# Where in 64 bytes the operands of the products begin: weights in one half, moving operands in the other

## The chip, the core and the metric

One core of one Trainium2 chip runs the whole kernel. The metric is the device time of one execution in microseconds, as the median of three runs. TensorE multiplies, VectorE and ScalarE do the elementwise work, GpSimd does little here, and all weights come from HBM by DMAs that SyncE issues.

## The reference

Two layers of a diffusion transformer over 256 tokens ("latents") and 256 context tokens of width 1024, in float32. Cut to what matters:

```python
for i in range(2):
    mod = silu(c) @ ada_w[i] + ada_b[i]             # six vectors; another six for the context
    h = rms_norm(x, g) * (1 + scale) + shift        # for x and for ctx
    y = even_mixer(h) if i == 0 else retention_mixer(h)
    x = x + gate * y                                # ctx likewise, in layer 0 only
    x = x + gate2 * (square(relu(h2 @ w1)) @ w2)    # h2: a second norm and modulation
return rms_norm(x, final_g)
# even_mixer: p = h @ w_in; a long convolution (by DFT products) on 3 x 512 columns,
#   attention in windows with 8 heads of 64; both @ w_out
# retention_mixer: p = h @ w_in; 4 heads, q and k of 256, v of 512, forwards and backwards;
#   o = (q k^T * decay) v, normalised, times silu(gates); @ w_out
```

## The kernel before

The tokens lie along the columns, 256 latents and then 256 context tokens; features lie across the 128 partitions. Every large product is split in two parts: a float32 operand is rounded to the type fp32r (`hi`) and the rest is kept as a second fp32r tile (`lo`), so that one product becomes three matmuls (`mm3`, line 149): hi x hi, hi x lo, lo x hi. `mm` gives TensorE a stationary operand (`lhsT`, 128 columns, loaded by an instruction of its own ahead of each matmul) and a moving one (`rhs`, 128, 256, 258 or 512 columns).

Weights arrive as 234 units of 128 x 1024 floats in the order of `unit_list`; `make_unit` (line 192) copies a raw unit into `wh` on ScalarE and the rest into `wl` on VectorE. The stages follow each other in time: the even mixer (to about 265 us; in it `hy` holds the modulated input, hi and lo tiles alike), the first MLP (`hx`, `hy` hold its input, `hid` its inner layer; 512 columns each, to about 640), the odd stage with the retention (to about 980), and the last MLP with the final norm (only the 256 latents; its input has 258 columns, since two columns carry the shift). Nearly always the weights are stationary. In the odd stage's `values` and `gates` it is the other way round: `hx`, `hy` are stationary and `wh`, `wl` move. In `scores` of the odd stage `kh`, `kl` are stationary and `qh`, `ql` move, and in `outs` `sh`, `sl` are stationary and `vh`, `vl` move. The order of instructions on TensorE is written out by hand in the mixers and around the norms; elsewhere a planner orders them by priorities.

Where a tile begins: a pool hands out addresses within a partition in the order in which its tags are first asked for, each tile rounded up to 32 bytes; the pools lie one behind the other. So every tile begins either in the first or in the second 32 of 64 bytes. In the program before, these are the halves:

- The pool `keep` (line 1428 on) has an odd number of 32-byte pieces before the pools that follow it, so `raw`, `wh`, `wl`, `nq` and the first tiles of each stage's pool begin in the second half. All tiles of the even stage that enter its fp32r products do, and all of the first MLP.
- In the odd stage `hx` and `hy` begin in the second half. The tile `lg` (8 floats, 32 bytes) turns that over for what is allocated after it: `qh`, `ql`, `kh0`, `kl0`, `kh1`, `kl1`, `vh`, `vl`, the four `sh`/`sl`, `sg` and `yth`, `ytl` begin in the first half.
- The last MLP takes its tiles from the same pool by the same tags. Its `hid` lies in `qh` to `vl`, in the first half. Its input lies in the tags of `hx`, `hy`, and there one slice of 258 floats is 1032 bytes long, so the four slices of a tile begin 32, 40, 48 and 56 bytes into their 64.

Slices of weights are 128 columns, 512 bytes, apart, so they begin in the half in which their tile does.

Of the kernel before, what the change touches and what calls it, by code (L numbers as in the profile page):

```python
# [9 lines left out]
F32 = mybir.dt.float32  # L10
F32R = mybir.dt.float32r
# [5 lines left out]
P = 128  # L17
D = 1024
KT = 8
SEQ = 256  # L20
TOK = 512
D_FF = 4096
EPS = 1e-6
# [33 lines left out]

CST = {}
_n = 0
for _name, _w in (("ident", 128), ("tneg", 2), ("wf", 2)):  # L60
    CST[_name] = (_n, _n + _w)
    _n += _w
N_CST = _n

# [63 lines left out]
class Build:  # L130
# [26 lines left out]

    def lo(self, o, x, hi, eng=None):
        return self.tt(o, x, hi.bitcast(F32), ALU.subtract, eng)

    def psm(self):
        return self.ps.tile([P, 512], F32, tag="m", name="psm", bufs=3)
# [232 lines left out]
    def norm_late(self, layer, sh, sc, h, part):  # L395


        lat = slice(0, SEQ)
        mod = self.mod[layer]
        dg = self.nq()  # L400
        self.V.memset(dg[:, SEQ : SEQ + 2], 1.0 / P)
        for i, (hi, lo) in enumerate(self.h_whole):
            x, y = (z.rearrange("p (k t) -> p k t", k=4)[:, :, SEQ:] for z in (hi, lo))
            shift = mod[:, sh, 4 * i : 4 * i + 4, :]
            self.S.copy(x, shift)
            self.lo(y, shift, x)
        with self.tc.high_priority(NORM_PRIO):
            for kt in range(KT):
                r, c = self.res[:, kt, lat], mod[:, sc, kt, 0:1]
                self.S.activation(h[kt][0][:, lat], r, AF.Copy, scale=c)  # L410
                self.V.scalar_tensor_tensor(h[kt][1][:, lat], r, c, h[kt][0][:, lat].bitcast(F32), op0=ALU.mult, op1=ALU.subtract)
        acc = self.sums(SEQ, 6)
        with self.tc.manual_schedule(engines={mybir.EngineType.PE}):
            for j in range(3):
                part(j, None, (0, 1))
            sums = self.rstd_sums(self.rstd_parts(acc, 6, lat), lat, self.psd())
            part(3, None, (0, 1))
            with self.tc.high_priority(NORM_PRIO):
                self.diagonal(self.inv_sqrt(sums, 2, D), 2, dg)
            ps = self.psn()  # L420
            self.mm(ps[:, : SEQ + 2], self.ones, dg[:, : SEQ + 2], True, True)
            self.rms = self.tmp2.tile([P, SEQ + 2], F32, tag="diff", name="rms", bufs=1)
            with self.tc.high_priority(NORM_PRIO):
                self.S.copy(self.rms, ps[:, : SEQ + 2])
# [128 lines left out]
    def mlp(self, layer, T, spread=0, pool=None):  # L553
        tc = self.tc
        with nullcontext(pool) if pool else tc.tile_pool(name="mlp", bufs=1, reuse_waits="tile") as pool:
            if layer == 0:
                self.tmp2, self.n_t2 = pool, T2_MLP
                self.cond = pool.tile([P, 2, 1024], F32, tag="cond", name="cond")
                self.nc.sync.dma_start(self.cond, self.I["ccrow"])
            TW = T if layer == 0 else T + 2  # L560
            h = self.h_tiles(pool, TW)
            self.T = T
            first = self.four()
            part = self.split_part(h, first)
            if layer == 0:
                self.norm_proj(layer, SH_M, SC_M, h, part)
            else:
                self.norm_late(layer, SH_M, SC_M, h, part)
            hid = {}
            end = self.last_mm  # L570
            if layer == 0:
                with tc.issue_after(self.last_act):
                    self.S.activation(self.cond, self.cond, AF.Silu)

            def evac(g, m, ps):
                if m == 0:
                    tags = [("hh", "hl")] * 2 if layer == 0 else MLP1_TAGS[g % 2]
                    hid[g] = [[pool.tile([P, 4 * T], F32R, tag=x, name="hid", bufs=1 if layer else 4) for x in pair] for pair in tags]
                hh, hl = hid[g][m // 4]
                sl = slice((m % 4) * T, (m % 4) * T + T)  # L580
                q = self.t2()
                if layer == 0:
                    r = self.t2()
                    self.S.activation(r[:, :T], ps[:, :T], AF.Relu)
                    self.tt(q[:, :T], r[:, :T], r[:, :T], ALU.mult)
                else:
                    self.tt(q[:, :TW], ps[:, :TW], self.rms, ALU.mult)

                def rest():
                    if layer:  # L590
                        self.S.activation(q[:, :T], q[:, :T], AF.Relu, bias=q[:, T : T + 1])
                        self.S.activation(q[:, :T], q[:, :T], AF.Square)
                    self.S.copy(hh[:, sl], q[:, :T])  # L593
                    self.lo(hl[:, sl], q[:, :T], hh[:, sl])

                return rest

            def w1(g):
                m0 = 0
                if g == 0:  # L600
                    m0 = 4
                    for rest in [evac(g, m, ps) for m, ps in enumerate(first)]:
                        rest()
                for m in range(m0, 8):
                    evac(g, m, self.proj_a(h, TW, self.psa() if layer and g == 0 and m < 6 else None))()
                    with self.tc.issue_after(end), self.tc.issue_after(self.last_lo):
                        self.more(spread)

            def w2(g):
                hs = []  # L610
                for kt in range(8):
                    hh, hl = hid[g][kt // 4]
                    sl = slice((kt % 4) * T, (kt % 4) * T + T)
                    hs.append((hh[:, sl], hl[:, sl]))
                if layer and g == 3:
                    self.final(hs)
                    return
                for m in range(6 if g == 3 else 8):
                    self.add_res(self.proj_a(hs, T), layer, G_M, m, slice(0, T))
                    self.more(SPREAD2 - m % 2)  # L620
                if g == 3:
                    self.all_adas()
                    self.tail(hs, T, layer, G_M, (6, 7))

            w1(0)
            for g in range(1, 4):
                w1(g)
                w2(g - 1)
            w2(3)

    def h_tiles(self, pool, T):
        h = []
        self.h_whole = []
        for i in range(2):
            hh = pool.tile([P, 4 * T], F32R, tag=f"hx{i}", name="hx")
            hl = pool.tile([P, 4 * T], F32R, tag=f"hy{i}", name="hy")
            self.h_whole.append((hh, hl))
            h += [(hh[:, j * T : j * T + T], hl[:, j * T : j * T + T]) for j in range(4)]
        return h


# [246 lines left out]
    def even(self):  # L888
        tc, nc, V, S, G, I = self.tc, self.nc, self.V, self.S, self.G, self.I
        with tc.tile_pool(name="even", bufs=1, reuse_waits="tile") as pool0:  # L890
# [6 lines left out]
                    return pool0.tile(shape, dt, tag=tag, name=name, bufs=self.bufs.get(tag, 1))  # L897

            pool = Sized()
            self.tmp2, self.n_t2 = pool0, T2_EVEN  # L900
            self.rope = pool.tile([P, 2, SEQ], F32, tag="rope", name="rope")
            self.mask = pool.tile([P, 2, P], BF16, tag="mask", name="mask")
# [69 lines left out]
            with tc.manual_schedule(engines={mybir.EngineType.PE}):  # L972
# [48 lines left out]
                def spectra():  # L1021

                    raw = self.raw(I["dft2"])
                    tabs.extend(pool.tile([P, 1024], F32R, tag="pt", name="dft") for _ in range(2))
                    S.copy(tabs[0], raw)
                    self.lo(tabs[1], raw, tabs[0])
                    self.all_adas()
# [38 lines left out]
            y = {}  # L1066
# [129 lines left out]
    def odd(self, stop=False):  # L1196
        tc, nc, V, S, G, I = self.tc, self.nc, self.V, self.S, self.G, self.I
        with tc.tile_pool(name="odd", bufs=1, reuse_waits="tile") as pool:
            self.tmp2, self.n_t2 = pool, T2_ODD
            h = self.h_tiles(pool, TOK)  # L1200
            rope = pool.tile([P, 6, SEQ], F32, tag="rope", name="rope1")
            nc.sync.dma_start(rope, I["rope1"])
# [1 line left out]
            nc.sync.dma_start(diff, I["diff"])  # L1204
            tri = pool.tile([P, 2, P], F32, tag="tri", name="tri")
            nc.sync.dma_start(tri, I["tri"])
            lg = pool.tile([P, 8], F32, tag="lg", name="lg")
            r0 = PAR["rate"][0]
            banks, part = self.qk_part(h)
            self.norm_proj(1, SH_A, SC_A, h, part)  # L1210
# [17 lines left out]
            def heads_qk(hd):  # L1228
# [5 lines left out]
                else:  # L1234
# [2 lines left out]
                qh = pool.tile([P, 2, 2, SEQ], F32R, tag="qh", name="qh")  # L1237
                ql = pool.tile([P, 2, 2, SEQ], F32R, tag="ql", name="ql")
                k = [
                    (pool.tile([P, 2, TOK], F32R, tag=f"kh{d}", name="kh"), pool.tile([P, 2, TOK], F32R, tag=f"kl{d}", name="kl"))  # L1240
                    for d in range(2)
                ]
                pair = lambda: self.t2().rearrange("p (a b) -> p a b", a=2)
# [36 lines left out]
            def scores(hd, q, k):  # L1280
                out = []
                for d in range(2):
# [7 lines left out]
                        blocks = [(pa, 0, 0, (0, 256), 0), (pa, 256, 1, (128, 256), 0), (pb, 0, 2, (0, 256), 256), (pb, 256, 3, (0, 256), 128)]  # L1290
                    else:
                        blocks = [(pa, 0, 0, (0, 128), 384), (pa, 128, 1, (0, 256), 256), (pb, 0, 2, (0, 256), 128), (pb, 256, 3, (0, 256), 0)]
                    sh = pool.tile([P, 896], F32R, tag=f"sh{d}", name="sh")
                    sl = pool.tile([P, 896], F32R, tag=f"sl{d}", name="sl")
                    for half in range(2):
                        s = self.t2()
                        for ps, c, kt, (q0, q1), e0 in blocks[2 * half : 2 * half + 2]:
# [122 lines left out]
    def run(self, stop=None):  # L1420
# [3 lines left out]
        with ExitStack() as es:  # L1424
# [13 lines left out]
            self.res = keep.tile([P, KT, TOK], F32, tag="res", name="res")  # L1438
            self.ones = keep.tile([P, P], F32, tag="ones", name="ones")
            V.memset(self.ones, 1.0)  # L1440
            self.eps = keep.tile([P, 1], F32, tag="eps", name="eps")
            V.memset(self.eps, EPS)
            self.csil = keep.tile([P, KT, 32], F32, tag="csil", name="csil")
            V.memset(self.csil, 0.0)
            self.nsink = keep.tile([P, 8], F32, tag="nsink", name="nsink")
# [75 lines left out]
def constants():  # L1521
# [4 lines left out]
    for t in range(2):  # L1526
        cst[:, CST["tneg"][0] + t] = -((np.arange(P) + P * t).astype(f4) / f4(SEQ))
        w = np.full(P, 2.0 / 512)
        if t == 0:
            w[0] = 1.0 / 512  # L1530
        cst[:, CST["wf"][0] + t] = w
    c["cst"] = cst

    t = np.arange(256)
# [120 lines left out]
```

## Time and profile before

| | |
|---|---|
| median of 3 runs | 1172.65 us (1171.71 to 1175.13) |
| profiled execution | 1174.92 us, span 1173.1 us |
| mean granted clock of TensorE | 0.997 |
| TensorE busy | 1146.3 us, 98%, 6922 matmuls |
| weight loads | 980.2 us, 84%, 6922 |
| VectorE busy | 797.4 us, 68% |
| ScalarE busy | 533.2 us, 45% |
| DMA | 181.77 MB, mean 155 GB/s |

A matmul's own duration in the profile reaches from its start to its modelled end, and successive matmuls overlap. The distance between their starts is what adds up; it is read from an unbroken piece of work with its count of instructions.

### The profile page before, as it was taken

The page shows a single profiled execution, that of the slowest core. Times are in us where ns is not written, and L with a number is a line of the kernel's source. Part 1 is how long each engine was busy: PE and PEld are TensorE (multiplying, and loading weights), DVE is VectorE, ACT ScalarE, POOL GpSimd, SP SyncE. Part 2 cuts the span into 40 slices and gives each one's busy share as a digit, 9 for nine tenths or more (in the row PEclk, how much of TensorE's full clock was granted, in tenths as well). Part 3 has the DMA queues.
Part 4 walks back from the last instruction along what each step waited for, and adds up shares of the span by engine and source line. Part 5 has one row for each costly group of instructions (what it writes and reads, how often), then busy time and mean ns, then how long its engine had stood idle before and what let it go on. Part 6 is the DMA issues. An engine that isn't in the chain of part 4 may idle for free.

```text
span 1173.1 us, 17557 instructions
## 1 busy us (share of the span) xinstructions
PE 1146.3 (98%) x6922; PEld 980.2 (84%) x6922; DVE 797.4 (68%) x1364; ACT 533.2 (45%) x840; POOL 33.6 (3%) x29
## 2 busy tenths in 40 slices
PE   6899999999999999999999999999999999999997
PEld 3566677789888888788889889889889889999997
DVE  5767666768999866666348847647647567766665
ACT  6455555336433132123236453453453545846544
POOL 1200000300000000000000000000000000000000
PEclk9999999999999999999999999999999999999999
DMA  8735545123676766665323343343342345555651
GB/s 305 265 91 155 187 132 172 54 73 116 213 221 213 244 205 207 198 197 179 96 88 133 112 144 109 109 143 104 112 144 73 126 125 171 185 185 183 189 186 54
DMA packets 50355, 181.77 MB, mean 155 GB/s; under 512 B 5601, under 2 KB 6177, under 8 KB 50146
## 3 DMA queue, kind: packets, MB, share of 16 engines
q1 hardware_dynamic: 49986, 180.14, 47.5%
q8 instruction: 54, 0.88, 0.3%
q10 hardware_dynamic: 288, 0.52, 0.1%
q14 instruction: 27, 0.22, 0.1%
HBM read 179.59 MB, written 1.05 MB: 154 GB/s over the span
## 4 chain that ended last, share of the span: by engine, by line
PE 85%; DMA 6%; DVE 5%; ACT 2%; issue 1%; SPq 0%; DVEq 0%; ACTq 0%
PE psm L146 65%; PE psa L146 13%; DMA raw<-in_adat 5%; PE psn L146 2%; PE psd L213 1%; DMA raw<-in_w 1%; DVE wl L156 1%; DVE ac L278 1%; DVE hy L393 1%; PE psa L1126 1%; PE psd L146 1%; PE psn L1187 1%; PE psa L1171 1%; ACT wh L198 1%; DVE t L156 1%
## 5 line engine op out<-in xcount | busy, mean ns | idle before, releaser
L198 ACT CAST wh<-raw 128x1024 fp32r<-128x1024 f32 x234 | 245.5, 1050 | 340.0 <-PE psm L146 237.9
L156 DVE TENSOR_TENSOR wl<-raw,wh 128x1024 fp32r<-128x1024 f32 x234 | 286.7, 1226 | 154.6 <-ACT wh L198 146.1
L146 PE MATMUL psm<-hy,wh 128*128 128x512 f32 (+2 forms) x952 | 304.9, 341 | 6.0 <-DVE hy L393 3.0
L146 PE MATMUL psm<-hid,wh 128*128 128x256 f32 (+1 forms) x1056 | 250.2, 330 | 0.1
L146 PE MATMUL psm<-hx,wl 128*128 128x256 f32 (+2 forms) x696 | 221.3, 318 | 0.8 <-DVE wl L156 0.8
L146 PE MATMUL psm<-hx,wh 128*128 128x256 f32 (+2 forms) x696 | 221.7, 319 | 0.1
L146 PEld LDWEIGHTS psm<-hy,wh 128*128 128x128 f32 x952 | 178.8, 190 | 28.3 <-DVE hy L393 5.2
L146 PEld LDWEIGHTS psm<-hid,wh 128*128 128x128 f32 x1056 | 178.1, 188 | 19.3 <-issue 0.5
L146 PE MATMUL psm<-hid,wl 128*128 128x256 f32 (+1 forms) x528 | 174.0, 330 | 0.3 <-DVE wl L156 0.3
L146 PEld LDWEIGHTS psm<-hx,wl 128*128 128x128 f32 x696 | 131.6, 189 | 10.2 <-DVE wl L156 1.5
L146 PEld LDWEIGHTS psm<-hx,wh 128*128 128x128 f32 x696 | 131.9, 190 | 9.5 <-ACT hx L385 0.5
L278 DVE SCALAR_TENSOR_TENSOR ac<-raw,cond 128x1024 f32<-128x1024 f32 x80 | 96.6, 1220 | 45.0 <-DMA raw<-in_adat 42.9
L146 PEld LDWEIGHTS psm<-hid,wl 128*128 128x128 f32 x528 | 99.3, 188 | 10.1 <-DVE wl L156 0.8
L484 DVE SCALAR_TENSOR_TENSOR res<-psm,mod,res 128x256 f32<-128x256 f32 x108 | 48.9, 481 | 62.2 <-PE psm L146 61.8
L146 PE MATMUL psm<-wl,hx 128*128 128x512 f32 x224 | 87.5, 391 | 0.0
L146 PE MATMUL psm<-wh,hy 128*128 128x512 f32 x224 | 87.2, 391 | 0.0
L146 PE MATMUL psm<-wh,hx 128*128 128x512 f32 x224 | 84.1, 391 | 0.0
L593 ACT CAST hid<-t 128x512 fp32r<-128x512 f32 (+1 forms) x64 | 32.5, 510 | 68.3 <-DVE t L156 67.6
L146 PE MATMUL psm<-hy,wl 128*128 128x512 f32 x128 | 50.7, 396 | 0.0
L146 PEld LDWEIGHTS psm<-wl,hx 128*128 128x128 f32 x224 | 42.1, 188 | 8.7 <-DVE wl L156 0.3
L146 PEld LDWEIGHTS psm<-wh,hy 128*128 128x128 f32 x224 | 41.9, 188 | 8.5
L146 PEld LDWEIGHTS psm<-wh,hx 128*128 128x128 f32 x224 | 41.8, 188 | 8.2
(323 smaller groups left out, 1593.9 us busy)
## 6 DMA issues: line engine op xcount, KB each, us to landing
raw<-in_w SPq DMA_DIRECT2D x234, 512.0 KB, 3.4
raw<-in_adat SPq DMA_DIRECT2D x56, 512.0 KB, 3.9
raw<-in_ada SPq DMA_DIRECT2D x40, 512.0 KB, 4.3
res<-in_x SPq DMA_DIRECT2D x4, 512.0 KB, 5.4
cond<-in_ccrow SPq DMA_DIRECT2D x1, 1024.0 KB, 5.7
rope<-in_rope SPq DMA_DIRECT2D x1, 768.0 KB, 5.3
dftraw<-in_dft SPq DMA_DIRECT2D x1, 512.0 KB, 6.7
raw<-in_dft SPq DMA_DIRECT2D x1, 512.0 KB, 4.5
```

The source lines that it names most:

```text
L146: return self.PE.matmul(o, lhsT=lhsT, rhs=rhs, start=start, stop=stop)
L156: return (eng or self.V).tensor_tensor(o, a, b, op=op)
L198: self.S.copy(hi, src)
L213: self.PE.matmul(ps[32 * j : 32 * j + 32, 0:n], lhsT=self.csil[:, kt, :], rhs=rhs, start=kt == 0, stop=kt == 7, tile_position=(0, 32 * j),)
L278: self.V.scalar_tensor_tensor(junk, src, 1.0, self.cond[:, i], op0=ALU.mult, op1=ALU.mult, accum_out=self.mod[layer][:, vec, kt, i : i + 1])
L393: self.last_lo = self.V.scalar_tensor_tensor(h[1][:, s], t[:, s], b, h[0][:, s].bitcast(F32), op0=ALU.add, op1=ALU.subtract).ins
L484: self.V.scalar_tensor_tensor(r, ps[:, s], self.mod[layer][:, vec, m, i : i + 1], r, op0=ALU.mult, op1=ALU.add)
L593: self.S.copy(hh[:, sl], q[:, :T])
L1126: self.PE.matmul(pss[u][:, cols], lhsT=self.qs[t][a][half[u], o : o + P], rhs=k[b][half[u], keys], start=i == 0, stop=i == 2 and x == 2, t ...
L1171: self.PE.transpose(pt[:, kt * P : kt * P + P], p[:, kt * P : kt * P + P], self.ident)
L1187: self.PE.matmul(ps[half[u], cols], lhsT=vz[:, kt, half[u]], rhs=turned[u][:, kt if n == 4 else kt + 2], start=i == 0, stop=i == n - 1, ti ...
```

## The change

`eps` is no longer a tile of 32 bytes in `keep` but one more column of the constants `cst` (132 to 133 columns, the same number of 32-byte pieces). A helper `pad` allocates `OFF` = 8 floats (32 bytes) and clears them on GpSimd, which moves what is allocated after it by half of 64 bytes; it is called at the head of the even, the first MLP's and the odd stage's pool, and around `sh`/`sl`. `lg` takes the place of `nsink` instead of a tile of its own. `kh` and `kl` become rows with `OFF` floats at both ends; `dft` begins `OFF` floats into its tile. `h_tiles` rounds the length of a slice up to a multiple of 16 floats.

```diff
-for _name, _w in (("ident", 128), ("tneg", 2), ("wf", 2)):
+for _name, _w in (("ident", 128), ("tneg", 2), ("wf", 2), ("eps", 1)):
...
+OFF = 8
...
+    def pad(self, pool, tag="pad"):
+        self.G.memset(pool.tile([P, OFF], F32, tag=tag, name="pad"), 0.0)
...
# norm_late
-            x, y = (z.rearrange("p (k t) -> p k t", k=4)[:, :, SEQ:] for z in (hi, lo))
+            x, y = (z.rearrange("p (k t) -> p k t", k=4)[:, :, SEQ : SEQ + 2] for z in (hi, lo))
...
# mlp, layer 0; the same call in even (ahead of rope) and in odd (ahead of h)
+                self.pad(pool)
...
# h_tiles
+        T0, T = T, (T + 15) // 16 * 16
...
-            h += [(hh[:, j * T : j * T + T], hl[:, j * T : j * T + T]) for j in range(4)]
+            h += [(hh[:, j * T : j * T + T0], hl[:, j * T : j * T + T0]) for j in range(4)]
...
# even, spectra
-                    tabs.extend(pool.tile([P, 1024], F32R, tag="pt", name="dft") for _ in range(2))
+                    tabs.extend(pool.tile([P, 1024 + OFF], F32R, tag="pt", name="dft")[:, OFF:] for _ in range(2))
...
# odd
-            lg = pool.tile([P, 8], F32, tag="lg", name="lg")
+            lg = self.nsink
...
-                    (pool.tile([P, 2, TOK], F32R, tag=f"kh{d}", name="kh"), pool.tile([P, 2, TOK], F32R, tag=f"kl{d}", name="kl"))
+                    [
+                        pool.tile([P, 2 * TOK + 2 * OFF], F32R, tag=f"{x}{d}", name=x)[:, OFF : OFF + 2 * TOK].rearrange("p (a b) -> p a b", a=2)
+                        for x in ("kh", "kl")
+                    ]
...
+                    if hd == d == 0:
+                        self.pad(pool, "pads")
                     sh = pool.tile([P, 896], F32R, tag=f"sh{d}", name="sh")
                     sl = pool.tile([P, 896], F32R, tag=f"sl{d}", name="sl")
+                    if hd == 0 and d == 1:
+                        self.pad(pool, "pade")
...
# run
-            self.eps = keep.tile([P, 1], F32, tag="eps", name="eps")
-            V.memset(self.eps, EPS)
+            self.eps = self.cst[:, CST["eps"][0] : CST["eps"][1]]
```

## Rows read from the trace of the kernel before

**Rows 1.** The page: busy time by engine, and the chain that ended last.

```profile
PE 1146.3 (98%) x6922; PEld 980.2 (84%) x6922; DVE 797.4 (68%) x1364; ACT 533.2 (45%) x840; POOL 33.6 (3%) x29
...
PE 85%; DMA 6%; DVE 5%; ACT 2%; issue 1%; SPq 0%; DVEq 0%; ACTq 0%
```

**Rows 2.** TensorE's waits, the longest first: waited for, us in total, times, longest us.

```profile
PE psa L146 <- DMA hyp<-in_hyp: 4.2, 1, 4.2
```

**Rows 3.** TensorE's groups by form: output, moving and stationary tile, shape, count, busy us, mean ns.

```profile
L146 PE MATMUL psm<-hy,wh 128*128 128x512 f32 x480 | 171.5, 399 | 5.8 <-DVE hy L393 3.0 <-ACT hy L385 2.7
...
L146 PE MATMUL psm<-hy,wl 128*128 128x512 f32 x128 | 50.7, 396 | 0.0
...
L146 PE MATMUL psm<-hid,wh 128*128 128x256 f32 x576 | 102.3, 281 | 0.0
...
L146 PE MATMUL psm<-hx,wh 128*128 128x256 f32 x240 | 68.8, 287 | 0.1
...
L146 PE MATMUL psm<-hy,wh 128*128 128x258 f32 x232 | 65.2, 281 | 0.0
...
L146 PE MATMUL psa<-qh,kh 128*128 128x256 f32 x48 | 13.7, 285 | 0.0
```

**Rows 4.** The chain in order of time: start us, length us, what, count.

```profile
292.49 152.13 PE psm L146 x671
...
655.92 4.13 PE psm L146 x18
...
668.02 4.39 PE psm L146 x19
672.41 1.42 PE psa L146 x12
...
679.57 3.45 PE psm L146 x15
...
709.73 10.19 PE psm L146 x85
719.92 8.49 PE psa L146 x72
```

**Rows 5.** Timeline in the first MLP: start us, length us, engine, what.

```profile
560.45 0.39 PE L146 MATMUL psm<-hid,wl 128*128 128x512 f32 x1
560.45 0.41 PEld L146 LDWEIGHTS psm<-hid,wh 128*128 128x128 f32 x2
```

**Rows 6.** Stretches: us, busy us of each engine, TensorE's granted clock, DMA share, GB/s.

```profile
25.00:200.00 175.00, 168.58 (x1031) 116.54 (x1030) 119.79 (x251) 89.77 (x181) 9.45 (x6) 0.99 0.49 166
292.50:352.00 59.50, 59.50 (x264) 49.23 (x264) 58.05 (x90) 24.64 (x37) 0.00 (x0) 1.00 0.72 218
352.00:381.00 29.00, 29.00 (x130) 24.01 (x129) 28.08 (x48) 8.96 (x11) 0.00 (x0) 1.00 0.69 212
528.00:617.00 89.00, 88.64 (x421) 74.69 (x421) 44.67 (x67) 26.46 (x33) 0.00 (x0) 1.00 0.38 124
1027.00:1118.00 91.00, 91.00 (x771) 91.00 (x771) 60.71 (x82) 53.50 (x81) 0.00 (x0) 1.00 0.57 186
```

**Rows 7.** The chain again, asked for three stretches of the last MLP.

```profile
998.91 29.15 PE psm L146 x243
...
1027.94 21.12 PE psm L146 x181
...
1118.93 30.10 PE psm L146 x258
```

**Rows 8.** Timeline of the start: memsets, and the first uses of `eps` and `cst`.

```profile
0.74 0.18 POOL L1449 MEMSET mod<- 128x96 f32 x1 [0.29 <-POOLq L1645]
...
2.03 0.20 ACT L704 ACTIVATE pre<-eps 128x1 f32<-128x1 f32 x1
...
3.23 0.23 DVE L920 CAST identb<-cst 128x128 bf16<-128x128 f32 x1
...
4.23 1.06 ACT L710 ACTIVATE row<-row 1x1024 f32<-1x1024 f32 x1 [0.94 <-DMA row<-in_hyrow]
```

More of the change, by code (lines that the diff above doesn't have):

```diff
@@ L899, in even @@
             pool = Sized()
+            self.pad(pool)
             self.tmp2, self.n_t2 = pool0, T2_EVEN
@@ L1199, in odd @@
             self.tmp2, self.n_t2 = pool, T2_ODD
+            self.pad(pool)
             h = self.h_tiles(pool, TOK)
@@ L1531, in constants @@
         cst[:, CST["wf"][0] + t] = w
+    cst[:, CST["eps"][0]] = EPS
     c["cst"] = cst
```

## The prediction

> **What bounds the kernel now.** I began with the busy times by engine and the chain that ended last. TensorE is busy for 98% of the span, and 85% of the chain is its work [rows 1]. Its waits are few: the longest of all, at the very start, is 4.2 us [rows 2]. So the time is the number of matmuls times the distance from one start to the next, and the views to read next are those that give this distance. The list by form gives a matmul's duration (396 ns for 512 columns, 281 for 256 [rows 3]), which is no help: matmuls overlap. The chain in order of time is, since one piece of it is an unbroken row of matmuls with their count. In 152.13 us there are 671 matmuls of 512 columns, so 226.7 ns each; 85 of 256 columns take 10.19 us, 119.9 ns each [rows 4]. The two differ by 106.8 ns for 256 columns, 0.417 ns a column, which is one column per cycle at 2.4 GHz, the level that was granted (1.00 in the stretches of [rows 6]). What is left is 13.2 ns per matmul at either width: 226.7 - 213.5 and 119.9 - 106.7. It does not grow with the columns, so I read it as something paid once per instruction or once per weight load.
>
> The weight loads lie beside the matmuls: the load for the next one starts within 10 ns of a matmul's start [rows 5]. At 256 columns both sides of TensorE are busy for all 91.00 of 91.00 us; in a stretch that is nearly all 512 columns the loads fill 74.69 us of 89.00 [rows 6].
>
> Now the contrast that decides. In the kernel before, weights and nearly all moving operands begin in the second half of 64 bytes. One large stage is different by accident: the second products of the last MLP stage, where `hid` lies in the first half and `wh`, `wl` in the second. There 181 matmuls take 21.12 us and 258 take 30.10 us, 116.7 ns each, at the same 256 columns [rows 7]. The first products of that MLP, 258 columns in steps of 1,032 bytes that wander through the halves, need 29.15 us for 243, 120.0 ns [rows 7]. And `yth`, `ytl` (first half) with `wh`, `wl` make 72 in 8.49 us, 117.9 ns, against the 119.9 of the piece just ahead of it, where both lie in the second half [rows 4]. So with opposite halves a matmul of 256 columns starts 2.0 to 3.2 ns sooner.
>
> **The change, part by part.** Which operands move: without `eps` the `keep` pool is 32 bytes shorter, and `raw`, `wh`, `wl`, `nq` pass to the first half. A pad in front of each stage's pool puts `hx`, `hy`, `ch`, `cl`, `zt` and the first MLP's `hid` back where they were, in the second. Without `lg` the odd stage's later tiles (`qh`, `vh`, `sg`, `yth`, the last MLP's `hid`) pass to the second half; the slices by `OFF` and the pads keep `kh`, `kl`, `sh`, `sl` in the first. So every fp32r product over 128 rows gets opposite halves; the attention's scores (`hi`, `lo`, 64 rows) keep equal ones.
>
> First term, 256 columns: the odd stage's q and k products (three forms of 240 and three of 16), and two tails of 96, 960 in all [rows 3]: 960 x 3.2 ns = 3.1 us. The retention's scores, three forms of 48, run 12 in 1.42 us, 118.3 ns [rows 4]: 144 x 1.6 = 0.2 us. Second term, the 768 of 258 columns (three forms of 232 and three of 24): from 120.0 to 116.7 plus two columns of 0.417, 117.5 ns: 768 x 2.5 = 1.9 us. The 768 of the last MLP's second products and those with `yth`, `ytl` had opposite halves already: nothing. Together 5.2 us.
>
> Third term, 512 columns: nine large forms hold 2,448 and smaller ones some 500, 2,950 in all [rows 3]. No stretch of the trace has 512 columns with opposite halves for long, so this price is bounded from both sides. Below: if all that isn't columns went, 13.2 ns each, 39 us. Above: after a change of stage the 512-column rows run less evenly for a while, 18 in 4.13, 19 in 4.39 and 15 in 3.45 us, 229.4 to 231.1 ns [rows 4]; were that the lasting rhythm, each would lose 4.3 ns, 12.7 us in all. I take the 3.2 ns of the 256-column rows. It is the nearest row, the same pair of operands differing in the half alone, and the 13.2 ns of which it is a part is the same at both widths. 2,950 x 3.2 = 9.4 us.
>
> The edits around them: each of the five pads is a memset of 32 bytes a partition on GpSimd, beside one of 0.18 us for 384 bytes [rows 8], on an engine that is busy 3% of the span [rows 1]; nothing waits for them, and nothing if they were late. `eps` now comes with `cst`: ScalarE's first use of it, at 2.03 us, moves to where VectorE first reads `cst`, 3.23 us, and pushes the two short activations behind it by some 0.5 us; the next one waits for its own transfer until 4.23 us after 0.94 us of idling [rows 8], so that idling hides it, and it would cost those 0.5 us at most if the row came sooner. `lg` in `nsink` waits for readers that ended with the attention: 0, and no gain. The two extra columns of tables, the longer rows of `h` and the copies of `norm_late` have the sizes they had.
>
> What could be late next is VectorE: it is busy 58.05 of 59.50 and 28.08 of 29.00 us in the first MLP [rows 6]. The new rhythm would shorten those 88.5 us by 1.4%, 1.2 us, and VectorE has 2.4 us spare; I count half of the 1.2 as lost. From 25 to 200 us TensorE idles 6.4 us for others [rows 6], so a little of the gain there goes into waits: 0.5 us.
>
> Sum: 5.2 + 9.4 - 1.1 = 13.5 us. The profiled execution took 1174.92 us (span 1173.1 and 1.8 around it), so 1161.4 by its clock. It was 2.3 us above the median of the three timed runs, 1172.65, which gives 1159.2: **1159 us**.
>
> **The rivals.** (B) Only 256 columns gain. For it: there the weight load fills all of the time [rows 6], so a conflict delays the load and with it the next matmul; at 512 columns the load has time to spare, and 226.7 ns may be set by something else. Against it: the equal 13.2 ns. Then 1172.65 - 5.2 = 1167.5 us.
>
> (C) At 512 columns most of the 13.2 ns goes, because there the conflict may be the whole of it. Half to all: 19.5 to 39 us, with the first two terms 1128 to 1148. Against it: at 256 columns only a quarter went. The Trainium skill, TensorE: Matmul & The Clock Gate, "Back-to-back issue gap", has 512 columns at N / 2.4 + 2.5, an estimate of 215.8 ns by that page; by it the gain at this width would be 10.9 ns each, 32 us, and no row here shows that rhythm.
>
> (D) Slower: at 512 columns the new halves never settle into 226.7 ns but keep the uneven rhythm of the starts of stages, 231.1 ns [rows 4]. That costs 12.7 us against the 5.2 gained: 1180. It decides from 228.5 ns a matmul on, where 1.8 x 2,950 eats the 5.2 us. For it: the smooth 226.7 is seen only with equal halves. Also, the gain is measured with the moving operand in the first half, and after the change it is mostly in the second; if only the one order gains, most of the first term is lost as well.
>
> (E) The halves don't do it, and TensorE reads its two operands without any conflict: 116.7 ns belongs to something else of that stage, such as where its tiles lie in a wider pattern. Then 1172 to 1174. For it: one stage and `yth` are all that show the contrast; against it: these two lie in different places and both start sooner than their neighbours, 116.7 and 117.9 against 119.9 ns [rows 4, 7]. This is also what the Trainium skill says, SBUF — State Buffer, "Who interferes with whom": TensorE has two independent read ports, one for the moving operand and one for the weights, and never waits on anyone. By that rule the time would stay at about 1172; the trace does not agree with it where it can be asked, by the same two pairs of numbers.
>
> **How the numbers follow.** My forecast 0.46 (1155 to 1163), B 0.17, C 0.10, D 0.15, E 0.12. The range 1145 to 1173 holds the forecast, B, most of E and the edge of C. A measurement of this kernel tells 0.3%, 3.5 us, from no change: faster is below 1169.1, slower above 1176.2. Forecast, C and most of B are faster, 0.70; E and a share of B and D the same, 0.15; most of D slower, 0.15.
>
> **What would show it.** The chain's long piece of 512 columns from 292 us: 223.5 ns each if right, 226.7 if B, below 220 if C, above 228.5 if D. The odd stage's rows of 85: 116.7 ns instead of 119.9. The first products of the last MLP: 117.5 instead of 120.0, and its second products unchanged at 116.7; if those grow, the order of the halves matters. The prediction is wrong if the 256-column rows gain and the 512-column rows don't, or if both gain and the span doesn't shrink by as much, in which case the waits of TensorE will have grown in the first MLP.

## The result: slower, and the profile after

The changed kernel takes 1187.20 us (median of 4 runs, 1185.96 to 1188.07) against 1172.69 for the kernel before: the ratio is 1.012, with a 95% interval of 1.0101 to 1.0139. The forecast was 1159, and the range ended at 1173. Rival D, slower, is what happened, and its price of 1180 was still too low.

The page of the changed kernel, with the busy times by engine and the engines' shares of the chain that ended last:

```profile
PE 1159.9 (98%) x6922; PEld 978.2 (83%) x6922; DVE 797.6 (67%) x1363; ACT 533.4 (45%) x840; POOL 34.0 (3%) x34
...
PE 94%; DVE 3%; ACT 2%; DMA 1%; issue 0%; SPq 0%; DVEq 0%; ACTq 0%
```

The number of matmuls is the same as in [rows 1], and nothing new waits: TensorE is busy for more time, and more of the chain is its own. In one stretch of the first MLP some idling has even gone: before, TensorE stood for 0.59 us between 450 and 528 us (77.41 busy of 78.00), now for none. So the distance from one matmul to the next must have grown. The chain of the changed kernel in order of time (start us, length us, what, count), the pieces that answer to [rows 4]:

```profile
292.13 331.79 PE psm L150 x1452
...
675.32 4.48 PE psm L150 x19
679.80 1.42 PE psa L150 x12
...
717.40 9.92 PE psm L150 x85
727.32 8.64 PE psa L150 x72
...
1009.79 150.69 PE psm L150 x1272
```

And the chain asked for the first MLP, the first products of the last MLP, and two stretches of its second products (the last three answer to [rows 7]):

```profile
299.83 120.40 PE psm L150 x516
```

```profile
1009.79 29.26 PE psm L150 x245
```

```profile
1038.94 21.09 PE psm L150 x180
```

```profile
1128.90 31.11 PE psm L150 x265
```

Read by width, length over count: 512 columns take 120.40 / 516 = 233.3 ns, where [rows 4] had 226.7. 256 columns in the odd stage's queries and keys take 9.92 / 85 = 116.7 instead of 119.9, as forecast. The 258 columns take 119.4 (120.0 before), the second products 117.2 to 117.4 (116.7 before), and the retention's output 120.0 (117.9 before). By place: from the start of the first MLP's long piece (292.49 before, 292.13 now) to the first row of 85 (709.73, now 717.40) the kernel loses 8.0 us, from there to the last MLP's long piece (998.91, now 1009.79) 3.2, and in that piece 0.2. Less the 0.4 us by which the first of these pieces starts earlier, that is the 11.2 us between the spans of the two profiled executions, 1173.1 and 1184.3, to 0.2 us. The execution of before was 2.3 us above its median and that of after 0.8 below, which makes up the 14.5 us between the medians.

The window of the fourth row of [rows 6] after the change (us, busy us of PE, PEld, DVE, ACT and POOL, clock, DMA share, GB/s): the clock is the same, and neither VectorE, ScalarE nor the DMAs do more than before. The two windows do not hold the same work: this one is all but two matmuls 512 columns wide, while that of before, which the prediction called nearly all 512 columns, has 358 of them and 60 of 256.

```profile
528.00:617.00 89.00, 89.00 (x384) 71.52 (x383) 41.06 (x61) 23.90 (x29) 0.10 (x1) 1.00 0.36 118
```

### The profile page after: what moved, and what is told of

It is laid out like the page before. It is cut to its first block, busy times and chain, and to the rows that moved or that the text cites. A ratio compares the mean times of both kernels' runs of the same rounds, so it can differ in the third digit from the quotient of the medians.

```text
span 1184.3 us, 17562 instructions
## 1 busy us (share of the span) xinstructions
PE 1159.9 (98%) x6922; PEld 978.2 (83%) x6922; DVE 797.6 (67%) x1363; ACT 533.4 (45%) x840; POOL 34.0 (3%) x34
## 4 chain that ended last, share of the span: by engine, by line
PE 94%; DVE 3%; ACT 2%; DMA 1%; issue 0%; SPq 0%; DVEq 0%; ACTq 0%
PE psm L150 73%; PE psa L150 13%; PE psn L150 1%; PE psd L221 1%; PE psa L1137 1%; PE psd L150 1%; ACT wh L206 1%; PE psn L1198 1%; PE psa L1182 1%; DVE wl L160 1%; DVE t L160 1%; DVE hy L401 1%; DMA raw<-in_w 1%; DMA res<-in_x 0%; PE psa L1188 0%
## 5 line engine op out<-in xcount | busy, mean ns | idle before, releaser
L150 PE MATMUL psm<-hid,wh 128*128 128x256 f32 (+1 forms) x1056 | 253.5, 333 | 0.0
```

Source lines behind the costliest of these rows:

```text
L150: return self.PE.matmul(o, lhsT=lhsT, rhs=rhs, start=start, stop=stop)
```

## The experiments

In what follows the distance is the moving operand's start minus the stationary one's, in bytes and modulo 256. In the kernel before it is 0 for every product of 512 columns over 128 rows, 0 for the queries and keys and for the retention's scores, and 32 for the last MLP's second products and the retention's output. In the changed kernel it is 32 for those that had 0, but 224 where the weights are the moving side and for the tables and the retention's scores against the values, and one of 32, 96, 160 and 224 for the scores themselves. The kinds that had 32 went to 96 (the retention's output) and to 32, 96, 160 and 224, tile by tile (the second products). The last MLP's first products, of 258 columns, went from 0, 8, 16 and 24 to 32, 96, 160 and 224, slice by slice.

**e1_grid.** Synthetic rows, 72 matmuls for each pair of places, one stationary and one moving tile whose bases lie 4,160 bytes apart.

```
for n in (512, 256): for s in (0, 16, 32, 48): for m in (0, 8, ..., 56):
    72 x matmul(p[:, :n], lhsT=st[:, (r % 8) * 128 + s / 4 ...], rhs=mv[:, m / 4 : m / 4 + n])
```

> The disputed cost by itself: this kernel computes nothing of the reference. One stationary tile of 8 slices of 128 columns and one moving tile, both fp32r; 72 matmuls in a row for each pair of starts, at 512 and then at 256 columns. The stationary slices begin 0, 16, 32 or 48 bytes into their 64, the moving ones 0, 8, 16, ... 56. Theory 1 (the distance from start to start is set by where the two operands begin relative to each other, and by the columns): 512 columns 226.7 ns with equal halves (0 and 0, 32 and 32) and 233.3 with opposite ones (0 and 32, 32 and 0); 256 columns 120.0 and 116.7. Theory 2 (the loss is due to something else that the change does, such as memsets, the new place of the constants, the absolute place of tiles): the same rhythm for all pairs, within 1 ns. What lies between the halves (8, 16, 24 bytes) neither tells; a start below 226.7 ns at 512 columns would be a better place for all stages.

Chain pieces of e1_grid (the name gives columns n, stationary place s and moving place m of 64 bytes); the rows follow each other without a pause, so length over count is the distance from start to start:

```profile
76.58 16.81 PE n512s0m32x L44 x72
...
126.59 17.27 PE n512s0m56x L44 x72
...
177.35 16.34 PE n512s16m16x L44 x72
...
344.19 16.48 PE n512s32m32x L44 x72
...
596.49 8.17 PE n256s0m48x L44 x72
```

512 columns take 233.5, 239.9, 226.9 and 228.9 ns in the first four, and 256 columns fall to 113.5 in the last. So places alone, with VectorE busy for 1% of the span and ScalarE for less, move the distance by 13 ns. But equal halves (s32m32) are not the even 226.7, and opposite ones are not one value either. The halves are too coarse a description. (The bases lie 64 bytes off each other modulo 256, so that s32m32 has a distance of 64.)

**e2_undo_512.** The changed kernel without the pads that move the first two stages' operands, so that 2,016 of the 512-column products and 384 of 256 columns are back at distance 0.

```diff
-                self.pad(pool)            # first MLP
-            self.pad(pool)                # even stage
-  pool.tile([P, 1024 + OFF], ...)[:, OFF:]
+  pool.tile([P, 1024], ...)               # tables
```

> The changed kernel without the pads at the head of the even and the first MLP's pool, and without the shift of the dft tables: there the operands pass to the first half, where the weights are, so 2016 matmuls of 512 columns and 384 of 256 columns have equal halves again; the odd stage and the last MLP stay as changed (936 of 512 columns opposite). Theory 1: 2016 x 6.6 ns = 13.4 us less and 384 x 3.3 = 1.3 us more than the changed kernel: 1187.2 - 12.1 = 1175. The long piece of the chain from 292 us is back at 226.7 ns a matmul. Theory 2: within 2 us of 1187.

Measured: 1177.32 us (1175.79 to 1178.77), 1.0036 of before (1.0024 to 1.0049), where theory 1 said 1175. The first MLP's long piece has the same 1,452 matmuls as in the changed kernel and is 9.05 us shorter, and the odd stage keeps its 9.92:

```profile
292.93 322.74 PE psm L150 x1452
...
709.21 9.92 PE psm L150 x85
```

So about 10 of the 14.5 us come and go with the places of the first two stages' operands, nearly all of it in the first MLP. The even stage gave nothing back: the piece behind it begins at 292.93 us here and at 292.13 in the changed kernel. That is most of what the expectation missed.

**e3_mirrored.** The changed kernel with a 32-byte tile less ahead of the weights, which moves all weights and operands by 32 bytes together: moving and stationary change halves, distances stay.

```diff
-  self.small.tile([P, 4], F32, tag="pre", name="pre")
+  self.small.tile([P, 4], F32, tag="pre", name="pre", bufs=1)     # at both places that ask for it
```

> The changed kernel with 32 bytes less in the pool of small tiles ahead of all others (tile pre has one buffer instead of two), so that every later tile passes to the other half: weights in the second, what moves in the first; each pair keeps opposite halves. Theory 1 (only the relation counts): as the changed kernel, 1187 within 2 us, 233.3 ns at 512 columns and 116.7 at 256. Theory 3 (the order counts: a moving operand in the second half is the bad one): the 2184 matmuls that move from the first half now go back towards 226.7 ns, up to 14 us less, 1173; the 768 with moving weights get worse.

Measured: 1186.62 us (1186.27 to 1188.27), 1.0113 of before (1.0096 to 1.013), as the changed kernel. The long piece is the same to 0.01 us:

```profile
294.11 331.79 PE psm L150 x1452
```

Which operand lies in which half does not matter here. Only their relation does, and the thought in rival D that one order might gain and the other lose falls.

**e4_triples.** The rows of e1_grid in the kernel's triples (high times high, high times low, low times high), with a pause ahead of each row.

```
lhsT, rhs = ((wh, hh), (wh, hl), (wl, hh))[r % 3]     # wl is wh + 4,224 bytes, hl is hh + 16,512
```

> As the first grid, with the kernel's own pattern: two stationary tiles, two moving tiles of 8 slices, three matmuls per slice (hi x hi, hi x lo, lo x hi), 96 in a row per pair of starts, and a pause of TensorE ahead of each row. Stationary slices begin 0, 16, 32, 48 bytes into 128, moving ones 0, 16, ... 112. It computes nothing of the reference. Theory 1 (halves of 64 bytes): 512 columns 226.7 ns where the two begin in equal places (also 64 bytes apart), 233.3 where 32 bytes apart; 256 columns 120.0 and 116.7. Theory 4 (the rhythm is one of several that the same places can fall into, chosen by what ran before; the first grid had 229 ns and 117.8 for the places that ran 226.7 and 120.0 in the kernel): after a pause each place falls into one rhythm, not the one by halves alone; places 16 bytes on (48 and 48) again give 226.7 and 113.3 as in the first grid.

No row of 512 columns settled at 226.7, not the equal places either: in the second half of each row its starts stood 228.8 to 233.4 ns apart (231.1 at s32m32). 256 columns stood at 116.6 to 120. Here the low tiles lay 128 bytes (modulo 256) off the high ones, which is not so in the kernel before. That led to the next run.

**e5_places.** The triples again, with the low tiles at whole multiples of 256 bytes from the high ones, and the distance the only variable.

```
[(512, 32, 0, 32 + d, 0, 2048) for d in (0, 8, ..., 64, 96, 128, 256, 512, 1024, 2048)] + ...
```

> As the second grid, now with all four tiles at the kernel's distances (multiples of 4096 bytes between hi and lo), since there the equal places did not give the kernel's 226.7 ns. Moving slices 0 to 2048 bytes off the stationary ones, hi and lo 128 bytes off each other, slices of 258 columns at steps of 1032, 1088 and 1152 bytes. It computes nothing of the reference. Theory 1 (halves of 64 bytes, nothing else): 226.7 ns at 512 columns wherever the distance is a multiple of 64, 233.3 at 32; 120.0 and 116.7 at 256. Theory 5 (the distance counts over a longer period, or between hi and lo): 226.7 and 120.0 only where the whole distance is a multiple of 4096, and not with hi and lo 128 bytes off, as in the second grid. Theory 4 (chosen by what ran before): neither; equal places again give 229 to 231 after a pause. At 258 columns a step of 1032 gives 120.0 by the kernel, 1088 the same as in the changed kernel (118.5 mean of both MLP products), 1152 is open.

Chain pieces of e5_places; s is the stationary place, m the moving one, l what the low tile lies off. Each row begins after a pause and its piece holds the uneven first gaps and the last matmul's end, so the lengths show the order, and the steady distance is taken from the starts of the second half of each row:

```profile
101.58 22.67 PE n512s32l0m64l0t2048x L50 x96
...
193.00 22.28 PE n512s32l0m96l0t2048x L50 x96
...
238.45 22.59 PE n512s32l0m160l0t2048x L50 x96
261.28 22.05 PE n512s32l0m288l0t2048x L50 x96
...
328.20 22.07 PE n512s32l0m2080l0t2048x L50 x96
...
463.60 22.48 PE n512s32l128m32l128t2048x L50 x96
...
579.84 11.48 PE n256s32l0m64l0t2048x L50 x96
...
699.37 11.79 PE n256s32l0m2080l0t2048x L50 x96
...
877.91 11.60 PE n258s32l0m48l0t1088x L50 x96
889.76 11.79 PE n258s32l0m64l0t1088x L50 x96
```

From place 32, at 512 columns a distance of 32 gives 233.33 ns, of 64 228.88, of 128 232.44, and of 0, 256, 512, 1,024 and 2,048 always 226.67. At 256 columns it is the other way round: a distance of 0 or any multiple of 256 gives 120.00, and 32 gives 116.67. These are the kernel's two numbers at each width, made with nothing but addresses. The halves of 64 were a special case of this: 32 is one of the distances that are not 0. The distance is not the whole rule, though: a distance of 0 gave 226.67 and 120.00 from places 0 and 32, but 231.12 and 118.33 from place 16 and 230.00 and 118.33 from place 48. The last two lines are slices of 258 columns at a step of 1,088 bytes: at distances of 32, 96, 160 and 224, those of the changed kernel, they take 119.4 ns (m64), and with 16 bytes less 117.79 (m48).

**e6_shift128.** The test of that in the kernel before: one pad of 128 bytes, which no half of 64 can notice.

```diff
             if layer == 0:
+                self.G.memset(pool.tile([P, 32], F32, tag="shift", name="shift"), 0.0)
```

> The kernel before with one tile of 128 bytes put at the head of the first MLP's pool, so that its operands (hx, hy, hid) lie 128 bytes further and every start stays in the half of 64 bytes in which it was. The distance from the stationary to the moving start turns from a multiple of 256 bytes into one of 256 plus 128 for 1,392 matmuls of 512 columns and 288 of 256 in that stage and for no other. Theory A (the halves of 64 bytes decide, equal halves give the even 226.67 ns at 512 columns): nothing changes, 1172.6 us, between 1171.5 and 1175. Theory B (the even 226.67 needs a distance that is a multiple of 256 bytes; the synthetic rows gave 233.33 and 232.44 at a distance of 128): 1,392 x 5.8 to 6.7 ns is 8.0 to 9.3 us more, less 288 x 1.4 ns, so 1180 to 1182 us, and the pieces of the chain in the first MLP go from 226.67 to 232 to 233.5 ns a matmul while those of the even and odd stages stay.

Measured: 1180.43 us (1179.76 to 1180.79), 1.006 of before (1.0042 to 1.0078). The first MLP's piece against the 671 in 152.13 of [rows 4], and the untouched odd stage:

```profile
290.21 156.17 PE psm L146 x672
...
715.23 10.19 PE psm L146 x85
725.42 8.49 PE psa L146 x72
```

156.17 / 672 is 232.4 ns, the value of the synthetic row at distance 128. 1,392 x 5.7 ns makes 7.9 us, where 7.1 were measured between the medians. Theory B said 1180 to 1182; theory A, the halves, said no change, and falls.

**e7_search.** Triples once more, to look for better places: the distance and the two offsets of the low tiles apart, 122 rows of 60.

> Synthetic rows of products, nothing of the reference is computed: 122 rows of 60 matmuls in triples of high and low parts, with the distance d from stationary to moving start and the distances of the low parts from the high ones chosen apart, all taken modulo 256 bytes. It looks for places that go below what the kernels have. Theory B's model that only the repeating cycle counts has no floor of its own: the one-operand rows gave 113.3 ns at 256 columns, the triples 116.7 and more. Expected: 256 columns between 113.3 and 121 with most rows between 117 and 120, and some below 116; 512 columns 226.67 only where all three distances are 0, otherwise 228 to 235; nothing at 512 columns under 226.6. If a row at 512 columns falls under 226, the fixed part is smaller than any row of the kernels shows.

Chain pieces of e7_search, 256 columns at distances 112 and 192 from place 0, and at 112 and 192 from place 48:

```profile
596.09 7.14 PE n256s0l0m112l0t2048x L46 x60
...
611.12 7.12 PE n256s0l0m192l0t2048x L46 x60
...
641.24 7.47 PE n256s48l0m160l0t2048x L46 x60
...
656.47 7.10 PE n256s48l0m240l0t2048x L46 x60
```

From the starts: 113.33, 113.36, 120.00 and 113.33 ns. So 192 gives 256 columns 113.3 ns from both places, where a distance of 0 had given 120.00 and 118.33 in e5_places, while 112 depends on the place itself. At 512 columns nothing came below 226.67, and that came only with all three distances at 0; the same 192 gave 233.31 there. The two widths want different places.

**e8_places_a and e9_places_all.** The kernel before with its products of 256 columns moved to 192, and those of 512 left at 0. e8 moves the last stages by one tile and an offset; e9 adds a start 64 bytes later for the weights of 24 units (its expectation says 32).

```diff
+            G.memset(pool.tile([P, 40], F32, tag="shift", name="shift"), 0.0)   # odd pool, behind h
-            hh = pool.tile([P, 4 * T], ...)
+            hh = pool.tile([P, 4 * T + O], ...)[:, O:]      # last MLP: step 320 columns, O = 48
...
-            hi = self.wp.tile([P, 1024], F32R, tag="wh", ...)     # e9 only, lo likewise
+            hi = self.wp.tile([P, 1088], F32R, tag="wh", ...)[:, o : o + 1024]    # o = 16 or 0
```

> The kernel before, with only the products of the last stages put at the distance of 192 bytes (modulo 256) at which the synthetic rows of 256 columns fell to 113.33 ns: a tile of 160 bytes in the odd pool moves hid of the last MLP (768 matmuls, 116.7 ns before) and yth (384, 118 ns before) there, and the last MLP's hx and hy begin 192 bytes into their tiles with a step of 1,280 bytes instead of 1,032 (768 matmuls of 258 columns, 120.0 ns before). The 512-column products keep a distance of 0. Theory B (only the distance counts, and each width has its own best one): 768 x 3.3 is 2.6 us, 384 x 4.6 is 1.8 us, and the 258 columns between nothing and 768 x 6 = 4.6 us, so 1163.5 to 1168.5 us. Theory A (halves of 64 bytes): hid and yth at opposite or equal halves of 64 are already at 116.7 and hx goes to no better place than the forecast gave it, 117.5 ns, so 1170 to 1173 us.

> The kernel of e8_places_a, and also the weights' halves of 32 units (odd queries and keys, the first MLP's first product, the two split tails) begin 64 bytes into their buffers, so that another 960 matmuls of 256 columns stand at a distance of 192 bytes (120.0 ns before) while all 512-column products keep 0. The weights' buffers are 256 bytes longer and one scratch tile of the first stage moved to another pool to make room; no instruction is added but the memset of the shifting tile. Theory B: 960 x 6.67 ns is 6.4 us less than e8_places_a, so 1157 to 1162 us, about 1 per cent under the kernel before; the odd stage's row of 85 goes from 10.19 us to 9.6 us and the 512-column row of 671 stays at 152.1 us. Theory A: distance 192 is an equal half, so these products stay at 120.0 and the time is that of e8_places_a.

e8: 1170.12 us (1168.70 to 1171.98), 0.997 of before (0.9959 to 0.9981). e9: 1168.22 (1166.62 to 1169.65), 0.9953 (0.9936 to 0.997). Both are faster than the kernel before, and both gained less than expected. e8's chain, with its retention's output and, asked for alone, the last MLP's first and second products:

```profile
708.35 10.20 PE psm L146 x85
718.54 8.18 PE psa L146 x72
```

```profile
996.12 29.59 PE psm L146 x245
```

```profile
1025.59 19.49 PE psm L146 x172
```

e9's chain, the same two rows of the odd stage:

```profile
707.11 9.65 PE psm L150 x85
716.76 8.48 PE psa L150 x72
```

256 columns did what the search promised in the second products, 113.3 ns (116.7 before), and only in part in the queries and keys. The row of 85 runs at 113.5 in e9 (119.9 before), but over the 960 products that e9 moved, pauses left out, the mean went from 121.2 to 117.6 ns, 3.4 us of the 6.4 expected. The 258 columns gained nothing: 120.8 in e8, where the expectation hoped for up to 6 ns. And the row of 72 shows what the model lacked. Its operands lie at the same addresses modulo 256 in e8 and e9, yet it runs at 113.6 ns in the one and 117.8 in the other. So a place allows more than one steady rhythm. Over all 384 products of the retention's output, whose mean is 114.0 ns in e8 and 116.4 in e9, that is 0.9 us of what e9 lacks.

**e10_256.** The changed kernel with all its edits, but pads of 256 bytes, and none around keys and scores: every distance is 0, save in the last MLP's first products, whose slices lie 0, 64, 128 and 192 apart from the weights.

```diff
-OFF = 8
+OFF = 0
-        self.G.memset(pool.tile([P, OFF], ...
+        self.G.memset(pool.tile([P, 64], ...
...
-                    if hd == d == 0:
-                        self.pad(pool, "pads")      # "pade" likewise
```

> The changed kernel with all its edits (the eps column, the step of 1,088 bytes, a memset for each pad) but with pads of 256 bytes instead of 32 and none around the keys and the scores: every product of 512 columns has a distance of 0 modulo 256 bytes again, and so have all of 256 columns, those of the last MLP's second product and of the retention's output too, which stood at 32 in the kernel before. Theory B: 512 columns back to 226.67 ns; 768 + 384 matmuls of 256 columns at 120.0 instead of 116.7 and 118 are 2.6 + 0.8 us over the kernel before, and the edits cost nothing, so 1175 to 1177 us. If the pads or the moved memsets themselves cost something, it stays above 1180. If equal halves were all that counts, the last MLP would still give 116.7 there or fall, and the time would be 1172 to 1173.

Measured: 1175.01 us (1173.81 to 1175.79), 1.002 of before (1.0006 to 1.0034), inside the expectation. The retention's output and, asked for alone, the last MLP's second products now run at 120.0 ns, where [rows 4, 7] had 117.9 and 116.7:

```profile
706.62 10.20 PE psm L150 x85
716.81 8.64 PE psa L150 x72
```

```profile
1025.91 20.16 PE psm L150 x168
```

The 768 and 384 that left a distance of 32 cost 2.5 + 0.8 us by these numbers, and 3.3 were measured between the medians, with an interval of 0.7 to 4.0: the edits themselves cost nothing that can be told from that.

**e11_step1088.** e9 with the last MLP's first operands at the place where e5_places had 117.79 ns for 258 columns.

```diff
-        S, O, T0 = (T, 0, T) if T == TOK else (320, 48, T)
+        S, O, T0 = (T, 0, T) if T == TOK else (272, 4, T)
```

> The kernel of e9_places_all with the last MLP's first operands at a step of 1,088 bytes and 16 bytes into their tiles instead of 1,280 and 192, the place where the synthetic rows of 258 columns had 117.79 ns. Theory B with places alone: 768 x (120.9 - 117.8) ns = 2.4 us less than e9_places_all, so 1165 to 1166.5 us. Rival: places only allow a set of repeating cycles and what ran before picks one, as in e9_places_all, where one place gave 113.4 in some rows and 117.8 in others; then 258 columns stay between 118 and 121 and the time between 1166 and 1168.5.

Measured: 1166.56 us (1164.98 to 1167.09), 0.9951 of before (0.9938 to 0.9964), against 0.9953 for e9: no difference. By the time alone the rival and theory B can't be told apart, for they meet at 1166.5. The first products, asked for alone, run 238 in 28.56 us, 120.0 ns (e9: 242 in 29.24, 120.8), and the second products behind them, at an unchanged place, 171 in 20.14, which is 117.8 against 113.4 in e9. Over the whole stage the first products gained 1.5 of the 2.4 us that theory B forecast, and the second lost 0.9:

```profile
992.50 28.56 PE psm L150 x238
```

```profile
1021.89 20.14 PE psm L150 x171
```

So places alone do not fix the rhythm, as the rival that was written down with it had it. Its reason, that what ran before picks the rhythm, is not shown. Up to the last MLP's first product TensorE has the same instructions at the same addresses in e9 and e11, and yet the last row of the retention's output, just ahead of that product, differs. In e9 and then in e11:

```profile
961.20 13.86 PE psa L150 x120
```

```profile
959.62 14.37 PE psa L150 x120
```

From start to start that is 114.1 and 118.4 ns. So neither the places nor the order of TensorE's instructions up to there decide it alone.

e9 and e11, 0.5% under the kernel before, are the best versions found.

## Why the prediction was wrong

**What bounds the kernel: right.** The time is the count of matmuls times the distance from start to start, and that distance moves when nothing but the operands' addresses is changed (e1, e5).

**The first term, 256 columns: right for the queries and keys.** The row of 85 runs at 116.7 as forecast; over the 960, pauses left out, the mean went from 121.2 to 118.4 ns, 2.7 us of the 3.1. The scores kept their 12 in 1.42 us.

**The second term, 258 columns: wrong.** The piece above shows 119.4 ns, and over all 768, pauses left out, the mean went from 120.0 to 119.8 ns, 0.1 us instead of 1.9. The subtraction took the four slices for one case, opposite halves. They lie at distances of 32, 96, 160 and 224, and e5_places gave 119.4 ns for such slices.

**The third term failed, and with it the sum.** The prediction took the 3.2 ns of the 256-column rows for 512 columns because the 13.2 ns above the columns were the same at both widths, and so read them as one fixed part. They are not one thing. At a distance of 0 both widths show about 13.3 ns above their columns, and at 32 the one has 10.0 and the other 20.0 (116.67 - 106.67, 233.33 - 213.33). The equality in the trace of before came from the distance 0 that both had there. Instead of gaining 3.2 ns each, 9.4 us, the 512 columns lost 6.7.

2,950 x 6.7 would be 19.7 us. The two profiled executions run the same 6,922 matmuls in the same order, so their distances can be compared one by one. 512 columns cost 14.0 us more, 256 columns 1.0 and 258 columns 0.1 less, and small products early in the first stage, which wait for others, 1.5 less: the 11.2 us between the spans to 0.1. What lacks of the 19.7 lies in three places. Up to the first MLP TensorE waits for others, and that MLP's long piece starts no later than before. In the first MLP the execution of before stood still six times, 1.7 us in all; e2 and e11 run its 512 columns at 226.7 ns without these pauses, so they belong to that execution and not to the places. And in the odd stage the 936 products of 512 columns ran at 228.5 ns before, not at 226.7, and at 233.0 after, pauses left out: 4.2 us and not 6.2.

**Nothing was to happen to the operands that had opposite halves already.** The retention's row of 72 went from 117.9 to 120.0 ns (1.0 us over all 384) and the second products from 116.7 to 117.3 (0.6 us over all 768). Their halves stayed opposite, but their distances modulo 256 moved from 32 to 96 and to 32 to 224, which the prediction did not look at; 96 gave 120.00 in e5_places.

**The edits: right, nothing** (e10). The loss of VectorE's cover did not come up, since the rhythm grew.

**The rivals.** D happened, at 233.3 where it priced 231.1; the prediction named its ground, that the smooth 226.7 had been seen only with equal halves, and gave it 0.15. E was wrong as put, but its aside on a wider pattern was right: the pattern is one of 256 bytes (e5, e6). No row in the trace of before could have told: every 512-column product over 128 rows had the same distance there, so there was no contrast at that width at all, and 0.46 for a term of 9.4 us with no row of its own was too much.

The Trainium skill, SBUF — State Buffer, "Who interferes with whom", gives TensorE two independent read ports. The runs agree only so far as no other engine was needed for the effect: in e1_grid, with VectorE busy for 1% of the span, two operands' addresses moved the distance, taken from the starts, between 113.3 and 130.0 ns and between 226.7 and 240.0.

**What stays open** is which part of the chip does this, why triples reach 226.7 ns only at multiples of 256 bytes while single pairs in e1 reach it elsewhere (s16m16), and what picks the rhythm. No run here sees into it.

## What to carry to other kernels

A quantity that is equal in two groups of rows is one cost only if something in the trace varies it; where all rows of one width share a condition, that width has no contrast and the term needs both ends in the range and a lower chance. Where TensorE is the bound, list the start addresses of both operands modulo 256 by width before moving any tile: pads that look free decide here between 226.7 and 233.3 ns. And test such a rule on synthetic rows with the kernel's own order of operands, and then on each stage, since the same places gave 113.6 and 117.8 ns in two kernels.

## What the runs showed of the hardware

- Starts of fp32r matmuls over 128 rows, at a granted clock of 1.00: triples of 512 columns 226.67 ns with moving, stationary and low tiles at multiples of 256 bytes from each other (from places 0 and 32 of 64; from 16 and 48 it was 231.12 and 230.00), otherwise 228.8 to 234.2 (e4, e5, e7); single pairs 226.7 to 240.0 (e1).
- Triples of 256 columns: 120.00 at a distance of 0 from places 0 and 32 (118.33 from 16 and 48), 116.67 at 32 from the same two, 113.33 at 192 from places 0 and 48 (and at 112 from place 0); with other distances or low tiles elsewhere 115.5 to 120.1 (e4, e5, e7).
- The same places can run in more than one even rhythm: a row of 120 products of 256 columns took 114.1 ns each in e9 and 118.4 in e11, behind the same TensorE instructions.
- After a pause it takes some matmuls until the even rhythm comes. In e5_places at a distance of 1,024 the gaps were 229, 233, 236, 224, 231, 236, 228, 233 and 230 ns, then 227, 227, 226 for the rest.
